# A Conformer mixer on one core: heads A in pairs of row halves, B's attention beside half of the output projection, norm factors on VectorE

## The chip, the cores and the metric

One Trainium2 chip, one core. The metric is the device time of one execution of the program, in microseconds. The trace comes from one profiled execution. Engines: PE is TensorE, PEld its weight loads, DVE VectorE, ACT ScalarE, POOL GpSimd; SP issues the loads.

## What is computed

One layer on a sequence of 512 tokens, width 1024, in float32:

```python
x = x + 0.5 * swiglu(rmsnorm(x), ffn1)
proj = rmsnorm(x) @ w_in                     # q, k, v of A (3 x 512), latents of B (256 + 128 + 32)
qa, ka = rmsnorm(heads of 64)                # A: 8 heads, bias by relative position, causal by chunks of 64
out_a = softmax(qa ka^T / 8 + bias) va
q  = rmsnorm(c_q) @ w_uq                     # B: 8 heads, 64 normed + 32 normed and rotated
kv = rmsnorm(c_kv) @ w_ukv                   # 64 of key, 64 of value; 32 rotated key columns are shared
out_b = softmax(q k^T / sqrt(96)) v          # the same chunk mask, no bias
x = x + concat(out_a, out_b) @ w_out
x = x + 0.5 * swiglu(rmsnorm(x), ffn2)
x = rmsnorm(x)
```

The feed-forward width is 2816. Every factor of a norm is 1 / sqrt(mean square + 1e-6).

## The kernel before

x is kept transposed, as 8 tiles of 128 columns by 512 tokens. Each matmul of float32 is made of three (`mm3`, L146 to L149): both operands are split into a high and a low part, and high x high, high x low and low x high are added in PSUM. The low part is made by a subtraction on DVE or POOL after a cast on ACT. Weights come in units of 128 x 1024 (`wunit`, L136): SP loads `raw`, ACT casts `whi`, POOL or DVE (`lo_on`) makes `wlo`; there are 4 buffers of each.

The mixer (L247 to L578) goes through these steps.

1. `in_proj` of the latents (L334), the factor of the row norm (L337 to L342), three latent norms with `factors` (L347 to L349).
2. `qk_proj` of qA (L377): 96 matmuls into four banks, squares on ACT, sums on DVE, `factors`, and a multiplication out of PSUM (L375). Then `latents_T`, B's queries (L384 to L404) and B's keys and values (L408 to L431), each with factors and scaling, with `rope` on POOL.
3. `qk_proj` of kA (L433), and `values_proj` for A (L566).
4. The heads, 8 of A and then 8 of B, in a software pipeline (L569 to L578). Iteration `it` flips the probabilities of head `it`, makes scores and softmax of head `it + 1`, prepares queries and keys of head `it + 2` (`front`), and multiplies the values of head `it - 1`. `front` transposes queries and keys on PE into the tag "tr", for A once for two heads, and splits them. `softmax` has four blocks of 128 queries with 512, 384, 256 and 256 columns: `mm3`, a reduction on DVE that adds the bias and finds the row's extreme (L522), an exponential on ACT (L524), a reciprocal on DVE (L525), a scaling on POOL (L526). `flip` (L529) transposes ten blocks into three banks of the tag "t" and splits them (L547, L548). A head of A has 64 rows: even heads lie in partitions 0 to 63, odd ones in 64 to 127.
5. After the pipeline, the output projection (L589 to L599): for each of 8 column blocks of x, 8 x 3 matmuls, a residual add (L595), a split for the second feed-forward part and a square sum. That part follows.

`rsqrt` (L112) is ln and exp on ACT and one Newton step of four DVE instructions. PSUM has eight banks; in the mixer 2 are for scores ("s"), 2 for transposes ("tr"), 3 for flips ("t") and 1 for values ("pv"). `bank` gives the projections four of them: group 0 is s, s, tr, tr and group 1 is t, t, t, pv.

The order on each engine is made by a planner (`schedule_with_timeline_sim`), which goes by the program's order, by its own estimate of each instruction's time and by priorities; `high_priority(offset=150)` moves the first fronts and softmaxes ahead (L572). Once it is made, each engine takes its instructions in that order. SP's queue holds the loads of weights and of the bias tables.

The lines that the steps below touch: L112 to L119, L276 to L289, L307 to L312, L358 to L433, L453 to L505, L507 to L527, L529 to L564, L569 to L578, L589 to L599.

Of the kernel before, what the change touches and what calls it, by code (L numbers as in the profile page):

```python
# [10 lines left out]
F32 = mybir.dt.float32  # L11
F32R = mybir.dt.float32r
AF = mybir.ActivationFunctionType
ALU = mybir.AluOpType
# [3 lines left out]
P = 128  # L18
# [12 lines left out]
BIG = 1e30  # L31

# [7 lines left out]
def tile_macaron_block(  # L40
# [206 lines left out]
    AH, AL = XH, XL  # L247
    with tc.tile_pool(name="mix", bufs=1, side="left", reuse_waits="tile") as mp:
        latT = mp.tile([P, 6, S], F32R, tag="vAh", name="latT")
        VBh = mp.tile([P, NT, 4, 192], F32R, tag="vBh", name="VBh")  # L250
# [22 lines left out]
        dve.tensor_scalar(out=nq[:, 0:1], in0=g(C_AQ), scalar1=-(HD ** -0.5), scalar2=None, op0=ALU.mult)  # L273
        dve.tensor_scalar(out=nq[:, 1:2], in0=g(C_BQ), scalar1=-(QK ** -0.5), scalar2=None, op0=ALU.mult)

        def factors(ss, n, width, scaled, name):  # L276

            f = mp.tile([P, NT, n], F32, tag="f_" + name, name="f_" + name)
            y = mp.tile([P, NT, n], F32, tag="y_" + name, name="y_" + name)
            y2 = mp.tile([P, NT, n], F32, tag="z_" + name, name="z_" + name)  # L280
            if scaled:
                dve.tensor_tensor(out=f, in0=ss, in1=vtok.unsqueeze(2).broadcast_to([P, NT, n]), op=ALU.mult)
                dve.tensor_scalar(out=f, in0=f, scalar1=1.0 / width, scalar2=EPS, op0=ALU.mult, op1=ALU.add)
            else:
                dve.tensor_scalar(out=f, in0=ss, scalar1=1.0 / width, scalar2=EPS, op0=ALU.mult, op1=ALU.add)
            rsqrt(f, f, y, y2)
            if scaled:
                dve.tensor_tensor(out=f, in0=f, in1=rtok.unsqueeze(2).broadcast_to([P, NT, n]), op=ALU.mult)
            return f  # L289
# [16 lines left out]
        with tc.tile_pool(name="ps2", bufs=1, space=PSUM, reuse_waits="tile") as ps:  # L306
            NB = {"s": 2, "tr": 2, "t": 3, "pv": 1}  # L307

            def bank(group, i, name):

                tag = (("s",) * NB["s"] + ("tr",) * NB["tr"], ("t",) * NB["t"] + ("pv",) * NB["pv"])[group][i]
                return ps.tile([P, 512], F32, tag=tag, name=name, bufs=NB[tag])  # L312

# [20 lines left out]
            pts = in_proj(0, LAT, 1)  # L334
            mt = bank(0, 3, "mt")
# [3 lines left out]
            yt = mp.tile([P, NT], F32, tag="yt", name="yt")  # L339
            zt = mp.tile([P, NT], F32, tag="zt", name="zt")  # L340
# [400 lines left out]
```

## Time and profile before

| | |
|---|---|
| median of 3 runs | 996.65 us (996.12 to 996.72) |
| the profiled execution | 997.57 us |
| its span, first to last instruction | 995.8 us |
| TensorE's mean granted clock | 0.994 of 2.4 GHz |
| PE busy | 975.5 us (98%) |
| DVE / ACT / POOL busy | 390.5 / 391.9 / 579.6 us |

The span is 1.8 us shorter than the execution's own time. Matmuls are pipelined and their ends are modelled, so a busy PE can still be slower than it might be; the starts are measured, and so are the gaps that a row calls idle. In a row, "<-" after the bracket's time names what ended the wait. The first feed-forward part lasts until about 368 us, the mixer with its output projection until 622 us, the second feed-forward part until the end.

### The profile page before, as it was taken

Reading aid. Unit: us, or ns where it says so; the run is one execution under the profiler, and the core shown is the slowest. Engines: PE = TensorE matmul, PEld = TensorE weight load, DVE = VectorE, ACT = ScalarE, POOL = GpSimd, SP = SyncE. Lnnn points to the kernel's source line nnn. Section 1 sums busy time; section 2 is a strip of 40 time slices with the busy share of each in tenths; the row PEclk is TensorE's granted clock in tenths of the full one; section 3 lists DMA queues with packets and bytes.
Section 4 is the critical chain, followed back from the end, with each engine's and each line's share of the span. In section 5 each row is a group of like instructions: output and inputs, shape, how many; then the busy total and the mean of one; then the engine's idle time right before and its main releaser. Section 6 shows DMA issues by size and latency. Waiting matters only on the chain.

```text
span 995.8 us, 12076 instructions
## 1 busy us (share of the span) xinstructions
PE 975.5 (98%) x4579; PEld 812.1 (82%) x4579; DVE 390.5 (39%) x684; ACT 391.9 (39%) x661; POOL 579.6 (58%) x424
## 2 busy tenths in 40 slices
PE   9999999999999999898999999999999999999996
PEld 6888888888888889786778978888888888888886
DVE  7533333333121233866788845143333333200002
ACT  7533323232222236563778853343233232322321
POOL 4776666765555530385445567587666667645541
PEclk9999999999999999999999999999999999999998
DMA  6432223233233242220110062323322232333302
GB/s 233 145 109 86 102 89 106 85 106 95 83 102 93 89 141 75 85 64 1 32 33 2 1 212 88 103 86 106 102 88 99 93 104 80 101 96 95 101 16 85
DMA packets 29146, 89.90 MB, mean 90 GB/s; under 512 B 3488, under 2 KB 5664, under 8 KB 29088
## 3 DMA queue, kind: packets, MB, share of 16 engines
q1 hardware_dynamic: 28224, 88.34, 27.6%
q8 instruction: 36, 0.59, 0.2%
q10 hardware_dynamic: 864, 0.79, 0.2%
q14 instruction: 22, 0.18, 0.1%
HBM read 87.02 MB, written 2.10 MB: 89 GB/s over the span
## 4 chain that ended last, share of the span: by engine, by line
PE 89%; DVE 4%; ACT 3%; POOL 2%; issue 1%; DMA 1%; SPq 0%; POOLq 0%; ACTq 0%; DVEq 0%
PE gu L147 15%; PE gu L149 15%; PE gu L148 15%; PE dn L147 8%; PE dn L149 8%; PE dn L148 8%; PE pj L149 2%; PE pj L147 2%; PE pj L148 2%; PE wo L147 1%; PE wo L149 1%; PE wo L148 1%; PE t L542 1%; PE s L147 1%; PE tr L457 1%
## 5 line engine op out<-in xcount | busy, mean ns | idle before, releaser
L143 POOL TENSOR_TENSOR wlo<-raw,whi 128x1024 fp32r<-128x1024 f32 x138 | 324.2, 2350 | 153.3 <-ACT whi L142 152.5
L142 ACT CAST whi<-raw 128x1024 fp32r<-128x1024 f32 (+2 forms) x159 | 162.4, 1022 | 447.7 <-PE gu L148 244.8
L147 PE MATMUL gu<-x2h,whi 128*128 128x512 f32 x352 | 136.9, 389 | 0.0
L148 PE MATMUL gu<-x2l,whi 128*128 128x512 f32 x352 | 136.8, 389 | 0.0
L149 PE MATMUL gu<-x2h,wlo 128*128 128x512 f32 x352 | 136.8, 389 | 0.0
L148 PE MATMUL gu<-xl,whi 128*128 128x512 f32 x320 | 124.5, 389 | 0.0
L147 PE MATMUL gu<-xh,whi 128*128 128x512 f32 x320 | 124.5, 389 | 0.0
L149 PE MATMUL gu<-xh,wlo 128*128 128x512 f32 x320 | 124.5, 389 | 0.0
L162 POOL TENSOR_TENSOR us<-us,gs 128x512 f32<-128x512 f32 x44 | 57.6, 1310 | 108.7 <-DVE us L160 107.2
L161 DVE SCALAR_TENSOR_TENSOR gs<-th,gs 128x512 f32<-128x512 f32 x44 | 91.1, 2074 | 31.8 <-ACT th L159 31.8
L158 DVE TENSOR_TENSOR gs<-gu,rs 128x512 f32<-128x512 f32 x44 | 30.4, 691 | 175.9 <-PE gu L149 168.7
L191 DVE SCALAR_TENSOR_TENSOR x<-dn,x 128x512 f32<-128x512 f32 (+1 forms) x17 | 11.2, 660 | 193.9 <-PE dn L149 193.9
L148 PEld LDWEIGHTS gu<-x2l,whi 128*128 128x128 f32 x352 | 66.1, 188 | 13.8
L149 PEld LDWEIGHTS gu<-x2h,wlo 128*128 128x128 f32 x352 | 66.1, 188 | 13.8
L147 PEld LDWEIGHTS gu<-x2h,whi 128*128 128x128 f32 x352 | 66.1, 188 | 13.6
L149 PEld LDWEIGHTS gu<-xh,wlo 128*128 128x128 f32 x320 | 60.1, 188 | 12.6
L147 PEld LDWEIGHTS gu<-xh,whi 128*128 128x128 f32 x320 | 60.1, 188 | 12.5
L148 PEld LDWEIGHTS gu<-xl,whi 128*128 128x128 f32 x320 | 60.1, 188 | 12.3
L147 PE MATMUL dn<-h1h,whi 128*128 128x512 f32 x176 | 68.5, 389 | 0.0
L148 PE MATMUL dn<-h1l,whi 128*128 128x512 f32 x176 | 68.5, 389 | 0.0
L149 PE MATMUL dn<-h1h,wlo 128*128 128x512 f32 x176 | 68.5, 389 | 0.0
L160 DVE SCALAR_TENSOR_TENSOR us<-gu,rs 128x512 f32<-128x512 f32 x44 | 30.4, 690 | 64.9 <-PE gu L149 64.9
(327 smaller groups left out, 1864.5 us busy)
## 6 DMA issues: line engine op xcount, KB each, us to landing
raw<-in_gu SPq DMA_DIRECT2D x84, 512.0 KB, 3.6
raw<-in_dn SPq DMA_DIRECT2D x32, 512.0 KB, 3.5
raw<-in_dn SPq DMA_DIRECT2D x16, 384.0 KB, 3.1
raw<-in_w_in SPq DMA_DIRECT2D x12, 512.0 KB, 3.4
raw<-in_w_out SPq DMA_DIRECT2D x8, 512.0 KB, 4.3
x<-in_xT SPq DMA_DIRECT2D x8, 256.0 KB, 5.4
raw<-in_gu SPq DMA_DIRECT2D x8, 256.0 KB, 5.4
bias<-in_bias_tab SPq DMA_DIRECT2D x8, 256.0 KB, 2.7
```

Of the source, the lines that this page charges most:

```text
L142: act.copy(hi[:, :n], raw[:, :n])
L143: (lo_on or pool).tensor_tensor(out=lo[:, :n], in0=raw[:, :n], in1=hi[:, :n].bitcast(F32), op=ALU.subtract)
L147: pe.matmul(out, lhsT=ah, rhs=bh, start=start, stop=False)
L148: pe.matmul(out, lhsT=ah, rhs=bl, start=False, stop=False)
L149: pe.matmul(out, lhsT=al, rhs=bh, start=False, stop=stop)
L158: dve.tensor_tensor(out=gs, in0=gup[0], in1=rs, op=ALU.mult)
L160: dve.scalar_tensor_tensor(out=us, in0=gup[1], scalar=0.5, in1=rs, op0=ALU.mult, op1=ALU.mult)
L161: dve.scalar_tensor_tensor(out=gs, in0=th, scalar=1.0, in1=gs, op0=ALU.add, op1=ALU.mult)
L162: pool.tensor_tensor(out=us, in0=us, in1=gs, op=ALU.mult)
L191: dve.scalar_tensor_tensor(out=x[dt][:, h], in0=pt[:, h], scalar=0.5, in1=x[dt][:, h], op0=ALU.mult, op1=ALU.add)
L457: pe.transpose(pt[0:src(t).shape[1], t * P:(t + 1) * P], src(t), ident)
L542: pe.transpose(tt[:, o + i * P:o + (i + 1) * P], pi[i][:, j * P:(j + 1) * P], ident)
```

## The change

1. `rsqrt_small` makes a first guess by integer arithmetic on the bits and takes three Newton steps, all on DVE: ten instructions. `factors` uses it and takes several norms at once: the three latent norms together, B's two query norms together. ACT's ln and exp remain in the feed-forward parts alone.
2. The pipeline's first four entries are pairs of A's heads. `softmax` makes the scores of both heads of a pair block by block, a matmul of the low half of the rows and then one of the high half. All four blocks have one reciprocal, and POOL scales them after it. The bias is loaded once a head as before, and its sign is put into the reduction (`scale=-1.0`), so that L482 goes. `pb` moves from the weight buffers into parts of `rs` and `ssum`.
3. `flip` fills its three banks one after the other, with the copies of each behind its transposes.
4. A's half of the output projection (`out_a`) runs in the iterations of B's heads, with its weights loaded in iterations 4 and 5 (`weights_o`) into the space of A's values and keys. B's half follows, with the first two column blocks begun before the last head's values (`out_b`). x gets two adds for each column block.
5. PSUM's eight banks: s 2, tr 1, t 2, pv 1, and 2 of a new tag pj, for second score tiles, B's keys and projections.

The diff, cut to its core:

```diff
+        def rsqrt_small(out, v, w):
+            y, t = (mp.tile([P, 2 * NT * NH], F32, tag="rsq", name="rsq", bufs=2)[:, 0:w] for _ in range(2))
+            dve.tensor_scalar(out=y.bitcast(I32), in0=v.bitcast(I32), scalar1=-0.5, scalar2=RSQ, op0=ALU.mult, op1=ALU.add)
+            for i in range(3):
+                dve.scalar_tensor_tensor(out=t, in0=y, scalar=-0.5, in1=y, op0=ALU.mult, op1=ALU.mult)
+                dve.tensor_tensor(out=t, in0=t, in1=v, op=ALU.mult)
+                dve.scalar_tensor_tensor(out=out if i == 2 else y, in0=t, scalar=1.5, in1=y, op0=ALU.add, op1=ALU.mult)
...
-            rsqrt(f, f, y, y2)
+            flat = f.rearrange("p i t n -> p (i t n)")
+            rsqrt_small(flat, flat, w)
...
-            NB = {"s": 2, "tr": 2, "t": 3, "pv": 1}
+            NB = {"s": 2, "tr": 1, "t": 2, "pv": 1, "pj": 2}
...
-                tag = (("s",) * NB["s"] + ("tr",) * NB["tr"], ("t",) * NB["t"] + ("pv",) * NB["pv"])[group][i]
+                tag = (("t", "t", "pv", "pj"), ("s", "s", "tr", "pj"))[group][i]
...
-            fcq = factors(ssl[:, 0], 1, 256, True, "cq")
-            fkv = factors(ssl[:, 1], 1, 128, True, "ckv")
-            fkr = factors(ssl[:, 2], 1, 32, True, "kr")
+            fcq, fkv, fkr = factors([(ssl[:, 0], 256), (ssl[:, 1], 128), (ssl[:, 2], 32)], 1, True, "lat")
...
+            def weights_o(i):
...
+                raw = wraw.tile([P, 1024], F32, tag="raw", name="raw")
+                nc.sync.dma_start(out=raw, in_=w_out[0, i])
+                act.copy(hi, raw)
+                pool.tensor_tensor(out=lo, in0=raw, in1=hi.bitcast(F32), op=ALU.subtract)
+                B["o", i] = hi, lo
+
+            def out_a(dt):
+                hi, lo = B["o", dt // 2]
+                pt = ps.tile([P, 512], F32, tag="pj", name="woa", bufs=NB["pj"])
+                for c in range(4):
+                    cc = slice((dt % 2) * 512 + c * P, (dt % 2) * 512 + (c + 1) * P)
+                    mm3(pt, hi[:, cc], lo[:, cc], OUT[c][0], OUT[c][1], c == 0, c == 3)
+                dve.tensor_tensor(out=x[dt], in0=pt, in1=x[dt], op=ALU.add)
...
-                    nc.sync.dma_start(out=bias, in_=bias_tab[h])
-                    dve.tensor_scalar(out=bias, in0=bias, scalar1=-1.0, scalar2=None, op0=ALU.mult)
-                    pool.memset(bias[0:HD, S - HD:S], BIG)
+                    nc.sync.dma_start(out=bias, in_=bias_tab[2 * pr + e])
+                    pool.memset(bias[0:HD, S - HD:S], -BIG)
...
-                    mm3(so[:, 0:nn], qh[:, ii], ql[:, ii], kh[:, 0:nn], kl[:, 0:nn], True, True)
...
-                    dve.reciprocal(sm[:, i:i + 1], sm[:, i:i + 1])
-                    pool.tensor_tensor(out=pi[i], in0=pi[i], in1=sm[:, i:i + 1].broadcast_to([P, (i + 1) * P]), op=ALU.mult)
+                    if i > 0:
+                        tag = "pj" if i == 2 and len(heads) > 1 else "s"
+                        bk = [ps.tile([P, 512], F32, tag=tag, name=f"s{i}", bufs=NB[tag]) for _ in heads]
+                    so = [b[:, 256:512] if i == 1 else b[:, 0:nn] for b in bk]
+                    for j, (a, b) in enumerate(((0, 2), (0, 3), (1, 2))):
+                        for o, hd in zip(so, heads):
+                            pe.matmul(o, lhsT=hd[a][:, ii], rhs=hd[b][:, 0:nn], start=j == 0, stop=j == 2)
...
+                for pi, mn, sm in out:
+                    dve.reciprocal(sm, sm)
+                    for i in (3, 2, 1, 0):
+                        pool.tensor_tensor(out=pi[i], in0=pi[i], in1=sm[:, i:i + 1].broadcast_to([P, (i + 1) * P]), op=ALU.mult)
...
+            beside = {}
+            for i in range(4):
+                beside.setdefault(4 + i // 2, []).append(lambda i=i: weights_o(i))
+            for dt in range(KD):
+                beside.setdefault(5 + min(dt, 6), []).append(lambda dt=dt: out_a(dt))
+            fronts = [lambda pr=pr: front_a(pr) for pr in range(4)] + [lambda b=b: front_b(b) for b in range(NH)]
+            n = len(fronts)
...
+                    if it == n:
+                        B["wb"] = wunit(w_out[1, 0], 1024)
+                        for dt in range(2):
+                            out_b(dt, 4, KD - 1)
...
+                    for f in more[e * half:(e + 1) * half]:
+                        f()
+            for dt in range(2):
+                out_b(dt, KD - 1, KD)
...
-            hi, lo = wunit(w_out[dt], 1024)
-            pt = ps.tile([P, S], F32, tag="mm", name="wo")
-            for c in range(KD):
+            if dt > 1:
+                if dt % 2 == 0:
+                    hi, lo = wunit(w_out[1, dt // 2], 1024)
+                pt = ps.tile([P, S], F32, tag="mm", name="wo")
+                for c in range(4, KD):
```

`w_out` is laid out anew on the host to match (two halves of four units of 128 x 1024).

## Rows read from the trace of the kernel before

**Rows 1.** The page's section 1: busy us, share of the span, instructions
```profile
PE 975.5 (98%) x4579; PEld 812.1 (82%) x4579; DVE 390.5 (39%) x684; ACT 391.9 (39%) x661; POOL 579.6 (58%) x424
```

**Rows 2.** Windows: length, busy us of PE, PEld, DVE, ACT, POOL, clock, DMA
```profile
405.00:420.00 15.00, 12.04 (x64) 10.29 (x63) 10.82 (x20) 10.92 (x18) 3.37 (x6) 1.00 0.37 123
420.00:461.00 41.00, 41.00 (x186) 34.42 (x186) 29.76 (x69) 22.57 (x50) 35.09 (x31) 1.00 0.12 39
461.00:470.00 9.00, 4.81 (x21) 3.92 (x20) 4.94 (x11) 2.87 (x4) 0.97 (x3) 0.81 0.00 0
...
482.00:521.00 39.00, 38.29 (x237) 29.12 (x235) 33.85 (x116) 29.81 (x87) 20.11 (x43) 1.00 0.15 42
521.00:578.60 57.60, 56.36 (x374) 49.91 (x373) 47.98 (x170) 47.45 (x135) 30.84 (x59) 1.00 0.10 34
```

**Rows 3.** Timeline, kA's chain: start us, us, engine, line, out<-in, idle before
```profile
459.51 1.20 DVE L283 TENSOR_SCALAR f_ka<-f_ka 128x32 f32<-128x32 f32 x1
...
460.99 1.28 ACT L115 ACT_TABLE_LOAD   x1
...
462.54 0.19 DVE L116 TENSOR_TENSOR z_ka<-y_ka 128x32 f32<-128x32 f32 x1 [1.83 <-ACT y_ka L115]
...
463.66 2.48 DVE L375 TENSOR_TENSOR kA<-pj,f_ka 128x512 f32<-128x512 f32 x4
...
465.70 1.08 PE L457 MATMUL tr<-ident,qA 128*128 128x128 f32 x4 [4.19 <-DVE kA L375]
```

**Rows 4.** Tile wo: count, duration ns min/median/max, first and last start us
```profile
L147 PE MATMUL wo<-xh,whi x64: 389/389/397, 579.3 to 622.1; 128*128 128x512 f32 x64
```

**Rows 5.** Timeline of PE, scores of single heads of A
```profile
482.44 0.38 PE L542 MATMUL t<-ident,pa 128*128 128x128 f32 x2
482.75 0.38 PE L147 MATMUL s<-qk,qk 64*128 64x256 f32 x1
...
483.30 0.44 PE L542 MATMUL t<-ident,pa 128*128 128x128 f32 x2
...
486.22 0.50 PE L147 MATMUL s<-xh,xh 64*128 64x512 f32 x1
...
487.12 0.66 PE L457 MATMUL tr<-ident,kA 128*128 128x128 f32 x4
```

**Rows 6.** Tile t of the flips, 470 to 578 us, as rows 4
```profile
L542 PE MATMUL t<-ident,pa x112: 270/273/332, 482.4 to 575.8; 128*128 128x128 f32 x112
...
L547 ACT CAST PBh<-t x32: 244/310/387, 485.0 to 577.7; 128x128 fp32r<-128x128 f32 x16, 128x256 fp32r<-128x256 f32 x16
...
L548 DVE TENSOR_TENSOR PBl<-t,PBh x31: 265/292/425, 486.5 to 576.9; 128x128 fp32r<-128x128 f32 x16, 128x256 fp32r<-128x256 f32 x15
```

**Rows 7.** Timeline, qA's chain
```profile
413.69 0.17 DVE L283 TENSOR_SCALAR f_qa<-f_qa 128x32 f32<-128x32 f32 x1
...
417.80 0.19 DVE L288 TENSOR_TENSOR f_qa<-f_qa,rtok 128x32 f32<-128x32 f32 x1
...
418.77 0.50 PE L147 MATMUL pj<-whi,xh 128*128 128x512 f32 x1 [1.24 <-DVE qA L375]
```

**Rows 8.** Timeline, POOL and DVE in kB's chain
```profile
452.54 1.29 POOL L303 TENSOR_TENSOR rtmp<-rtmp 128x512 f32<-128x512 f32 x1
452.66 1.22 DVE L117 TENSOR_TENSOR z_kn<-z_kn,f_kn 128x32 f32<-128x32 f32 x1
```

**Rows 9.** Timeline of PE, scores of two heads of A
```profile
493.11 0.49 PE L147 MATMUL s<-xh,xh 64*128 64x512 f32 x2
...
493.99 0.33 PE L542 MATMUL t<-ident,pb 128*128 128x128 f32 x1
```

**Rows 10.** Lines by form, DVE, 470 to 578 us: count, busy, mean ns
```profile
L525 DVE RECIPROCAL sm<-sm 128x1 f32<-128x1 f32 x64 | 9.0, 151 | 1.3 <-ACT pb L524 0.6 <-ACT pa L524 0.5
...
L482 DVE TENSOR_SCALAR bias<-bias 128x512 f32<-128x512 f32 x6 | 3.6, 594 | 0.9 <-DMA bias<-in_bias_tab 0.9
```

**Rows 11.** The page's section 5, POOL's low part of a weight unit
```profile
L143 POOL TENSOR_TENSOR wlo<-raw,whi 128x1024 fp32r<-128x1024 f32 x138 | 324.2, 2350 | 153.3 <-ACT whi L142 152.5
```

More of the change, by code (lines that the diff above doesn't have):

```diff
@@ new lines, in norm_k @@
+            def norm_k():
+                fk, = factors([(B["ssk"], HD)], NH, False, "kn")
+                for t in range(NT):
+                    dv = kB[:, t, :].rearrange("p (h w) -> p h w", w=HD)
+                    pool.tensor_tensor(out=dv, in0=dv, in1=fk[:, t, :].unsqueeze(2).broadcast_to([P, NH, HD]), op=ALU.mult)
+            tiles_b()
+            for j in range(3):
+                latents_T(j)
+            for i in range(8):
+                queries_b(i // 4, i % 4)
+            norm_q()
@@ L436, in values_proj @@
+            for i in range(8):
+                keys_values_b(i // 2, i % 2)
+            norm_k()
+            qk_proj(416 + 512, kA, "ka", 1)
             def values_proj():
@@ new lines, in values, with out_b @@
+                    act.copy(oh, pv)
+                    dve.tensor_tensor(out=ol, in0=pv, in1=oh.bitcast(F32), op=ALU.subtract)
+            def out_b(dt, c0, c1):
+                if c0 == 4:
+                    B["b", dt] = ps.tile([P, 512], F32, tag="pj", name="wob", bufs=NB["pj"])
+                pt, (hi, lo) = B["b", dt], B["wb"]
+                for c in range(c0, c1):
+                    cc = slice(dt * 512 + (c - 4) * P, dt * 512 + (c - 3) * P)
+                    mm3(pt, hi[:, cc], lo[:, cc], OUT[c][0], OUT[c][1], c == 4, c == KD - 1)
+                if c1 == KD:
+                    dve.tensor_tensor(out=x[dt], in0=pt, in1=x[dt], op=ALU.add)
@@ new lines, in tile_macaron_block @@
+            for it in range(-2, n + 1):
+                pis = prob.pop(it, [None])
+                more = beside.get(it, [])
+                for e, pi in enumerate(pis):
+                    cur = None
+                    if pi is not None:
+                        cur = head, flip(pi)
+                        head += 1
+                    if e == 0:
+                        with (tc.high_priority(offset=150) if it < 0 else ExitStack()):
+                            if 0 <= it + 1 < n:
+                                prob[it + 1] = softmax(qk.pop(it + 1))
+                            if it + 2 < n:
+                                qk[it + 2] = fronts[it + 2]()
+                    if it == n:
+                        B["wb"] = wunit(w_out[1, 0], 1024)
+                        for dt in range(2):
+                            out_b(dt, 4, KD - 1)
+                    if last:
+                        values(*last)
+                    last = cur
+                    half = (len(more) + 1) // 2 if len(pis) > 1 else len(more)
+                    for f in more[e * half:(e + 1) * half]:
+                        f()
```

290 lines of the change are left out of this document (142 added, 148 removed).

## The prediction

> **What bounds the kernel now.** First the busy shares of the page: PE runs for 98% of the span [rows 1], so time can only come from work taken off PE or from holes in its stream. Then the stretches of the mixer [rows 2], where the reader is to see how few holes there are and who stands beside them. PE has 3.0 us idle in 405 to 420 and 4.2 us in 461 to 470, and the granted clock of the latter is 0.81: (1 - 0.81) x 9 us x 2 = 3.4 us at the lower level (1.2 of 2.4 GHz), behind a hole of 4.19 us [rows 3], which costs another 1.7 us of work. From 482 to 578.6, the attention, PE looks full, but matmul ends are modelled, so I count its work. The 192 matmuls of the output projection, 512 columns each, keep one pace: 64 of one line from 579.3 to 622.1 us [rows 4], 42.8 us for 189 steps, 226 ns each. The columns of one head's values (512, 384, 256, 256, three matmuls each, 4224 in all) are then 1.87 us; 16 heads of values and 8 of B's scores make 45 us, some 245 transposes at 0.11 us (0.38 us for two [rows 5], 0.27 us for one [rows 6]) 27 us, A's scores about 16 us. That is 88 of 96.6 us: some 8 us idle, with DVE at 87% and ACT at 76% in A's part (482 to 521), both at 83% in B's.
>
> I take a step's chain of waits from the timeline and a stage's cost from its busiest engine.
>
> **1. Norm factors by Newton steps.** Each chain loses two ACT instructions, mostly with a table load of 1.28 us ahead [rows 3], and goes from four DVE steps to ten. A dependent step takes 0.22 us: five of them from 462.54 to 463.66 us [rows 3]. Two chains reach PE.
>
> For qA, DVE's L283 starts at 413.69 and L288 at 417.80 [rows 7]: 4.1 us. Ten steps behind L283 are 0.2 + 10 x 0.22 = 2.4 us, 1.7 us sooner, more than PE's wait of 1.24 us at 418.77 [rows 7]. **-1.2 us**; bounds -3.0 (the whole hole) and +0.8 (steps held by POOL, below).
>
> For kA the old hop over ACT began early, and ten steps save only 0.5 us: L283 of this chain ended at 460.7, L375 starts at 463.66 [rows 3], where it would start near 463.2. But the two merged chains before it (three of the latents, two of B's queries) also lose their loads, so POOL's rope and key scaling, which follow, end sooner, and the table loads no longer stand between ACT's squares and casts. PE sat in front of the transposes although the projection of A's values was ready; the planner had put these first by its own estimate of the chain, and a chain on one engine should miss its estimate by less. I take half the hole, and with it half the time at the lower clock: **-2.5 us**; bounds -5.9 (hole and clock) and +1.0.
>
> Here the row speaks against the change: DVE's L117 took 1.22 us instead of 0.19 and ended as POOL's L303 ended [rows 8]. So each Newton step can cost a POOL instruction. The Trainium skill says the same (SBUF — State Buffer, "SBUF: two separate sides"): DVE and GpSimd share a port pair as an exclusive lock, held for a whole instruction. By that rule alone the term would be a loss; this is the third rival.
>
> **2. A's heads in pairs.** A head's scores have 64 rows, and a pair now issues low half, high half, low half. The serial price: 0.90 us for three matmuls of 512 columns (486.22 to 487.12), 0.55 us for three of 256 (482.75 to 483.30) [rows 5]; 384 columns lie between, 0.72 us. A head: 0.90 + 0.72 + 2 x 0.55 = 2.72 us, eight 21.8 us. The old kernel already shows the overlap: a block of 512 columns of one head and one of 256 of another, six matmuls, took 0.88 us (493.11 to 493.99) [rows 9], not 1.45, and the timeline has this six times, so the scores cost some 18.4 us now. In pairs, 4 x 2.72 = 10.9 us. A change into the 64-row form costs about 0.1 us (0.31 us from two transposes at 482.44 to the score, where two steps are 0.22 [rows 5]); some nine fewer give 0.9 us. In all 8.4 us of PE work are gone.
>
> What of it reaches the time? DVE loses six of eight reciprocals a pair (0.151 us each) and two bias negations (0.594 us) [rows 10]: 2.1 us. About three pairs run in 482 to 521, so DVE falls from 33.85 to 27.7 us, PE by some 6.4 us to about 30, and ACT, unchanged at 29.8 us [rows 2], becomes the fullest. The fullest engine fills 87% of the stretch today; 29.8 / 0.87 = 34.3, so -4.7 us, and -1.1 us for the pair that lies outside the stretch (half its PE saving). **-5.8 us**; bounds 0 and -8.4.
>
> One reciprocal for all four blocks means that POOL scales a head only after its last exponential. POOL's queue is half empty here (20.1 of 39 us), and the flip of these probabilities comes an iteration later: nothing, unless that lead is used up. The bias loads keep their number on SP.
>
> **3. A's half of the output projection beside B's attention.** 96 matmuls, 21.7 us, move from behind the attention into it. With them go four weight loads on SP, their ACT casts and POOL lows (2.35 us each [rows 11]), and eight extra residual adds on DVE (as wide as L375, 2.48 us for four [rows 3]: 5.0 us). B's part has 57.6 us, about 5 of them idle on PE (its share of the 8). New demand: PE 57.6 - 5 + 21.7 = 74.3; DVE 48.0 + 5.0 - 3.6 (24 reciprocals) = 49.4; POOL 30.8 + 9.4; ACT's casts fit into its 10 us of slack. With the others at two thirds, the latencies that made the holes are covered, and at the drain the first two blocks of B's half stand in. **-4.5 us**; bounds -5 (every hole) and +2. An add that waits for its matmuls holds the score reductions queued behind it on DVE, and POOL's 9.4 us stand ahead of the scaling: that is the +2. In the projection that is left, POOL has one low and two square sums (the shape of L303, 1.29 us [rows 8]) for 5.4 us of matmuls, 4.9 us: full, but it has been ahead of PE by then, so 0.
>
> **4. Banks.** PSUM's tiles become 2 for scores, 1 (not 2) for transposed queries and keys, 2 (not 3) for flips, 2 shared ones for second score tiles, B's keys and projections. I charge nothing: other heads' matmuls stand between in the queue. If that cover is gone it is the slower rival.
>
> **Sum.** -1.2 - 2.5 - 5.8 - 4.5 = -14.0 us. The profiled execution took 997.57 us (span 995.8 and 1.8 around it), so 983.6; it lies 0.9 us above the median of 996.65, so in the runs' measure **982.6 us**.
>
> **Rivals.**
> *All holes close.* -3.0 - 5.9 - 8.4 - 5 = -22.3: 974.4 us. For it: each is a wait with a named releaser, and out_a is work without waits. Against: ACT and DVE don't become faster.
> *Evacuation, not PE, sets A's pace.* The matmuls of a pair finish earlier but exponentials and low parts come no sooner, or the planner doesn't alternate the halves; A gives -2 (the DVE share), B -3, the rest as above: -8.7, 988 us. For it: ACT's 29.8 us. Against: it had 9 us of slack. The Trainium skill has this as a rule (TensorEngine Tiling (Array Packing), "PSUM Bottleneck": packing speeds TensorE, not the emptying of PSUM). The 87% of DVE bears it out in part.
> *Newton steps behind POOL.* In 420 to 461 POOL is busy for 35.1 of 41 us and DVE for 29.8 [rows 2]. The chains of B's queries and keys lie there: some ten of their twenty steps meet a POOL instruction, 1.0 us each [rows 8]. DVE has 11 us to spare, but the reductions and low weights of kA queue behind; if some 7 us come through, -14 + 7 = -7: 989.6 us.
> *Slower: flips wait for their banks.* With two banks, the third tile of a flip waits until the first is copied: two ACT copies of 0.31 us and two DVE lows of 0.29 us [rows 6], 1.2 us, less the 0.33 us of the second tile's transposes, 0.87 us; 16 heads 14 us. The single bank between queries and keys adds at least the same 1.2 us for 4 pairs: 5 us. -14 + 19 = +5: 1001.6 us. It decides where over three quarters of that is exposed, 0.65 us a flip. Against: rows 5 show the transposes already cut up between other heads' scores.
>
> **Chances.** Forecast 0.52, all holes 0.12, evacuation 0.16, Newton behind POOL 0.10, slower 0.10. Below 0.2% (2 us) a measurement of this kernel can't tell a change from none. Faster 0.86: the first three, and most of the fourth; same 0.04; slower 0.10. The range goes from just under the second case to above the third and fourth, 972 to 993; some 0.07 lies below, 0.12 above.
>
> **What would show it.** Right: no table loads between 386 and 465; L288 of kA less than 2.6 us behind its L283; score matmuls of two heads starting within 0.02 us of each other; a pair of A in 11.5 to 12 us; PE without holes while projection matmuls stand in B's part. Wrong: Newton steps of 0.6 to 2 us; flips' transposes whose wait names L548; score matmuls of the two halves 0.2 us apart; a wait longer than 3 us ahead of kA's transposes with the clock at half behind it.

## The result, and the profile after

The changed kernel takes 1010.08 us (median of 4 runs, 1009.49 to 1012.39) against 996.68 us before on the same chip: a ratio of 1.0136 with a 95% interval of 1.0117 to 1.0156, so 1.4% slower. The forecast was 982.6 us. The profiled execution took 1012.39 us, with a span of 1010.5 us.

Section 1 of the page, of after, answers to [rows 1]; PE and DVE are busy for a little longer, ACT and POOL for less, and PE's share falls from 98% to 97%:

```profile
PE 984.3 (97%) x4579; PEld 817.7 (81%) x4579; DVE 393.6 (39%) x660; ACT 373.4 (37%) x629; POOL 573.8 (57%) x424
```

To find the loss, I cut each span at four marks: the first matmul of the mixer's input projection, the first transpose of A's queries, the fourth evacuation of values (the last of A), and the first matmul of the second feed-forward part. The windows between them, of before (start to end, length, busy time and count of PE, PEld, DVE, ACT and POOL, granted clock, DMA share, GB/s):

```profile
367.80:465.70 97.90, 90.75 (x435) 78.71 (x433) 62.44 (x157) 56.31 (x109) 48.40 (x55) 1.00 0.22 72
465.70:539.50 73.80, 72.54 (x423) 57.22 (x424) 56.82 (x191) 51.48 (x145) 31.86 (x65) 0.98 0.08 22
539.50:622.80 83.30, 82.61 (x458) 71.25 (x457) 55.08 (x130) 50.35 (x117) 55.79 (x58) 1.00 0.28 92
```

The same windows of after:

```profile
366.50:464.00 97.50, 91.75 (x441) 79.89 (x439) 70.51 (x179) 36.18 (x77) 44.37 (x55) 0.99 0.25 72
464.00:550.50 86.50, 82.82 (x428) 64.47 (x429) 53.45 (x159) 53.64 (x146) 32.25 (x65) 0.83 0.08 25
550.50:636.50 86.00, 81.80 (x448) 69.39 (x447) 50.22 (x112) 48.69 (x112) 48.90 (x53) 1.00 0.24 74
```

The projections are 0.4 us shorter, A's part is 12.7 us longer, the stretch from there to the second feed-forward part 2.7 us, and that part, to the end of the span, 1.0 us (374.0 after 373.0). The mixer starts 1.3 us earlier. Together 14.7 us, the difference of the spans.

A's part has a granted clock of 0.83. Two stretches of after at the lower level (1.2 of 2.4 GHz), with the one just ahead of the second:

```profile
459.00:469.00 10.00, 5.97 (x19) 4.62 (x18) 5.87 (x14) 0.69 (x1) 1.56 (x4) 0.66 0.00 0
476.00:482.60 6.60, 5.00 (x32) 3.40 (x31) 5.99 (x22) 5.89 (x18) 0.00 (x0) 1.00 0.00 0
482.60:506.50 23.90, 23.90 (x79) 16.90 (x80) 11.40 (x37) 12.18 (x36) 11.96 (x24) 0.50 0.15 45
```

The first is (1 - 0.66) x 10 x 2 = 6.8 us long, the second 23.9 us. Before there were 3.4 us [rows 2]. At the lower level matmuls of 512 columns start 0.43 us apart instead of 0.23 (after, 466.13 and 466.56 against 469.73 and 469.95 us), so about half of such time is lost wherever PE has work. In A's part lie 28.8 us of it now and 2.7 us before, the rest in the hole ahead of the transposes: an estimate of 14.4 us lost now, 1.4 then. That is the 12.7 us of A's part and a little more: without the lower clock, A's part would be 72.1 us, where that of before would be 72.4.

What PE did before the clock fell the second time is in the timeline of PE, of after (start, us, engine, line, operation, out<-in, count, idle before and its releaser):

```profile
463.97 1.08 PE L504 MATMUL tr<-ident,qA 128*128 128x128 f32 x4 [4.03 <-DVE kA L375]
...
472.91 0.60 PE L504 MATMUL tr<-ident,kA 128*128 128x128 f32 x4
...
475.42 0.39 PE L151 MATMUL pj<-whi,xl 128*128 128x512 f32 x1
475.74 1.49 PE L577 MATMUL s<-qk,qk 64*128 64x512 f32 x9
...
478.03 0.62 PE L577 MATMUL s<-qk,qk 64*128 64x256 f32 x3 [0.21 <-DVE mn L579]
479.03 1.27 PE L577 MATMUL s<-qk,qk 64*128 64x256 f32 x6 [0.38 <-DVE mn L579]
480.56 0.65 PE L504 MATMUL tr<-ident,kA 128*128 128x128 f32 x4 [0.27 <-DVE xl L509]
...
482.60 1.11 PE L577 MATMUL s<-xh,xh 64*128 64x512 f32 x3 [0.74 <-ACT xh L508]
```

Three things are to be seen. The hole ahead of the transposes is still there, 4.03 us (4.19 us before, [rows 3]). The keys of the first pair are transposed 8.9 us after its queries, when the projection of A's values is all but used up, so the scores start with nothing left beside them. And the first flip comes only at 487.80 us, 12.1 us after the first score; before it was 9.2 us (473.2 to 482.4). Between 475.7 and 487.8 us PE has scores and transposes alone, each waiting for its evacuation.

### The profile page after: what moved, and what is told of

Read it like the earlier page. It is cut to its first block, busy times and chain, and to the rows that moved or that the text cites. A ratio compares the mean times of both kernels' runs of the same rounds, so it can differ in the third digit from the quotient of the medians.

```text
span 1010.5 us, 12006 instructions
## 1 busy us (share of the span) xinstructions
PE 984.3 (97%) x4579; PEld 817.7 (81%) x4579; DVE 393.6 (39%) x660; ACT 373.4 (37%) x629; POOL 573.8 (57%) x424
## 5 line engine op out<-in xcount | busy, mean ns | idle before, releaser
L145 POOL TENSOR_TENSOR wlo<-raw,whi 128x1024 fp32r<-128x1024 f32 x134 | 315.1, 2353 | 141.4 <-ACT whi L144 138.3
L144 ACT CAST whi<-raw 128x1024 fp32r<-128x1024 f32 (+2 forms) x155 | 158.0, 1020 | 435.1 <-PE gu L150 242.1
L585 POOL TENSOR_TENSOR pa<-pa,sm 128x512 f32<-128x512 f32 (+2 forms) x48 | 35.6, 756 | 59.6 <-DVE sm L583 59.6
```

The costliest lines, as they stand in the source:

```text
L144: act.copy(hi[:, :n], raw[:, :n])
L145: (lo_on or pool).tensor_tensor(out=lo[:, :n], in0=raw[:, :n], in1=hi[:, :n].bitcast(F32), op=ALU.subtract)
L585: pool.tensor_tensor(out=pi[i], in0=pi[i], in1=sm[:, i:i + 1].broadcast_to([P, (i + 1) * P]), op=ALU.mult)
```

## The experiments

All times stand against runs of the kernel before on the same chip, 996.2 to 998.0 us by the batch. The time of a single run can be off by 1 to 3 us (four runs of e14 lay between 988.47 and 991.65, five of e9 between 999.19 and 1002.80), so kernels that ran once (e1 to e4, e6 to e8, e11, e12, e15, e18) are read by the stages of their profile. The stages of every kernel, cut as above; "half" is the time at the lower clock between the first and the last mark, in us. Stages and "half" are those of the one profiled execution:

| kernel | time | proj. | A | B | FFN2 | half |
|---|---|---|---|---|---|---|
| before | 996.68 | 97.9 | 73.8 | 83.3 | 373.0 | 3.4 |
| after | 1010.08 | 97.5 | 86.5 | 86.0 | 374.0 | 30.7 |
| e1_serial | 1006.1 | 97.5 | 80.1 | 85.9 | 374.6 | 17.1 |
| e2_k_on_pj | 1003.75 | 97.5 | 77.4 | 85.9 | 374.6 | 10.2 |
| e3_wo_behind | 1009.42 | 98.4 | 85.6 | 85.9 | 372.4 | 30.7 |
| e4_ln_exp | 1010.32 | 98.0 | 83.8 | 86.0 | 374.1 | 27.3 |
| e5_newton_alone | 997.83 | 97.7 | 73.9 | 85.1 | 372.4 | 3.4 |
| e6_key_norm_late | 1004.53 | 93.1 | 83.8 | 85.9 | 374.2 | 23.9 |
| e7_flip_banks_3 | 1004.45 | 97.8 | 72.9 | 90.2 | 375.2 | 20.4 |
| e8_k_pj_recip_by_block | 994.36 | 98.3 | 71.9 | 81.2 | 374.4 | 3.4 |
| e9_recip_by_block | 999.63 | 97.6 | 77.9 | 81.2 | 374.6 | 13.6 |
| e10_pairs_held_together | 1032.97 | 97.5 | 112.0 | 81.2 | 374.1 | 54.5 |
| e11_r_wo_behind | 1000.58 | 98.4 | 75.2 | 84.4 | 373.0 | 6.8 |
| e12_r_heads_singly | 997.23 | 98.4 | 74.0 | 81.2 | 374.0 | 6.8 |
| e13_pairs_ordered | 996.10 | 97.5 | 74.6 | 81.2 | 374.6 | 6.8 |
| e14_three_edits | 989.97 | 93.1 | 72.4 | 81.1 | 374.6 | 0 |
| e15_flip_banks_3_recip | 992.93 | 97.9 | 68.9 | 84.1 | 374.6 | 10.2 |
| e16_four_edits | 988.39 | 93.8 | 66.0 | 84.0 | 374.6 | 0 |
| e17_three_edits_ordered | 991.79 | 94.7 | 73.0 | 81.2 | 374.5 | 6.8 |
| e18_three_edits_wo_behind | 992.15 | 93.1 | 74.1 | 84.4 | 372.8 | 0 |

### First batch: which part brings the lower clock

e1 takes the alternation of the two heads inside a block out, e2 puts kA's transposes in the shared banks, e3 moves A's half of the output projection back, e4 takes the factors by ln and exp again, still merged.

```diff
-                    for j, (a, b) in enumerate(((0, 2), (0, 3), (1, 2))):
-                        for o, hd in zip(so, heads):
+                    for o, hd in zip(so, heads):
+                        for j, (a, b) in enumerate(((0, 2), (0, 3), (1, 2))):
```

> The changed kernel, but in each block of a pair the three matmuls of one head come first and then the three of the other (no alternation of the row halves). Theory ramp (PE falls to half clock from 482.6 to 506.5 us because the scores of the first pairs stand behind A's values projection, with nothing else to multiply): the stretch at half clock stays, 15 us or more of it, and the time is 1009 to 1016 us. Rival rows (two 64-row matmuls beside each other are what lets the clock fall): the stretch at half clock is under 7 us and the time falls to 998 to 1003 us. Rival banks (flips wait for their two banks, the clock is a side effect): within 3 us of 1010.

```diff
-                evac(kh, kl, transposes(lambda t: kA[:, t, hs]), g(C_AK))
+                evac(kh, kl, transposes(lambda t: kA[:, t, hs], "pj"), g(C_AK))
```

> The changed kernel, but the transposed keys of A go into a bank of pj and no longer into the single bank tr behind the queries. Theory ramp: kA's transposes follow qA's at once, scores of the first pair mix with the values projection as in the kernel before, the time at half clock in 470 to 510 us falls from 24 to under 7 us, and the kernel takes 997 to 1002 us. Rival rows: half clock for 15 us or more all the same, 1006 us or more. Rival banks: 1007 to 1012 us, with the waits of values and flips for the copies as they are.

```diff
-            for dt in range(KD):
-                beside.setdefault(5 + min(dt, 6), []).append(lambda dt=dt: out_a(dt))
...
+            for c in range(KD):
+                hi, lo = wa[c // 4]
```

> The changed kernel without its third part: nothing of the output projection beside the attention, all of it after the last head (each x gets one add). A's part up to 520 us should stay as it is, half clock included, in every theory. If the move is worth what the prediction charged, 1014 to 1016 us; if it is worth nothing or costs (the adds on DVE and POOL's low parts in front of the softmax), 1005 to 1011 us.

```diff
-            dve.tensor_scalar(out=y.bitcast(I32), in0=v.bitcast(I32), scalar1=-0.5, scalar2=RSQ, op0=ALU.mult, op1=ALU.add)
...
+            rsqrt(out, v, y, t)
```

> The changed kernel with the norm factors by ln and exp on ACT and one Newton step again, still merged. Rival of the prediction, Newton steps behind POOL (four steps of the kA chain took 1.0 us each behind the scaling of kB): the hole ahead of kA's transposes (4.0 us) shrinks by 2 us or more, the half clock behind it shortens from 6.8 to 3.4 us, 1004 to 1008 us. If the chains cost the same both ways, 1008 to 1012 us.

e2 is the one that says most alone: 6.3 us. With a bank of their own, kA's transposes follow qA's at once, the first score comes at 471.6 instead of 475.7 us, beside the projection of A's values, and 30.7 us at the lower clock become 10.2. Its A part fell by 9.1 us. Behind 470 us 6.8 us at the lower clock are left, as theory ramp has it; the time lies 1.75 us above that theory's range. That the order of the heads in a block (e1) changes the clock as well, by 13.6 us of stretch, shows how little it takes at the start of the attention. e1's time and stretch fit none of its three theories: 1006.1 us, with 13.6 us at the lower clock behind the start. e3 and e4 changed nothing that can be measured: neither the moved projection nor the Newton steps by themselves bring the loss, and the hole ahead of the transposes was 4.26 us with ln and exp. Both times lie where their theory of no gain and no loss has them.

### Second and third batch: one part alone, and the reciprocal

e5 is the kernel before with the Newton factors and nothing else of the change; the new function and its calls are those of the diff above.

> The kernel before with the Newton factors alone (each chain by itself, the old order of the work, the old banks, heads singly). If the Newton steps are a gain and only the new order and banks lose (theory 'ramp and banks'): 993 to 996 us, no lower clock beyond the one 3.4 us stretch. If the steps held behind POOL cost time in themselves (theory 'Newton behind POOL'): 998 to 1001 us, with the hole ahead of the first transposes longer than the 4.19 us of before.

It took 997.83 us, a ratio of 1.0009 (0.9999 to 1.0019): no gain and hardly a loss, between both theories. Its stages are those of before within 0.2 us up to the end of A's part; B's part is 1.8 us longer in its profile and FFN2 0.6 us shorter. The hole ahead of its first transposes is 4.46 us, longer than the 4.19 us of before, as the second theory has it.

```diff
-            norm_k()
             qk_proj(416 + 512, kA, "ka", 1)
+            norm_k()
```

> The changed kernel with the norm factors and the scaling of B's keys issued behind the projection of kA instead of ahead of it, so that POOL's 4.05 us scaling no longer stands beside kA's Newton steps. Theory 'Newton behind POOL': the steps go from 1.0 to about 0.2 us, the hole ahead of the transposes shrinks from 4.03 to about 1 us, the stretch at half clock at 462 goes, and the time is 1004 to 1007 us. Theory 'the one tr bank and the evacuations empty PE at the change of stage': the hole goes, but the clock still falls near 480 for 10 us or more, and the time is 1007 to 1010 us.

The hole went, as the first theory has it, and the projections shrank by 4.4 us to 93.1. The clock then fell at 473.4 us for 23.9 us, as the second has it; the time, 1004.53 us, lies in the range of the first. Its first flip comes 12.1 us after its first score, exactly as in after.

```diff
-            NB = {"s": 2, "tr": 1, "t": 2, "pv": 1, "pj": 2}
+            NB = {"s": 2, "t": 3, "pv": 1, "pj": 2}
...
-            def transposes(src, tag="tr"):
+            def transposes(src, tag="pj"):
```

> The changed kernel with three banks for the flips again and none of its own for transposed queries and keys (these go to the two shared banks, where the score tiles of 384 columns, B's keys and the projections are). Theory 'flips wait for their two banks': waits of flip transposes for their copies nearly gone, B's part 4 to 6 us shorter, 1002 to 1006 us. Theory 'flips are late because their probabilities are': waits of flip transposes stay at over half, 1007 to 1012 us.

The time fits the first theory, but not by its mechanism: the gain is in A's part, 13.6 us, of which less time at the lower clock explains some 7.6, and B's part became 4.2 us longer, with two stretches of 3.4 us at the lower clock in it.

```diff
                         act.activation(pi[i], pi[i], AF.Exp, bias=mn[:, i:i + 1], scale=-1.0, accum_out=sm[:, i:i + 1])
-                for pi, mn, sm in out:
-                    dve.reciprocal(sm, sm)
-                    for i in (3, 2, 1, 0):
+                        dve.reciprocal(sm[:, i:i + 1], sm[:, i:i + 1])
                         pool.tensor_tensor(out=pi[i], in0=pi[i], in1=sm[:, i:i + 1].broadcast_to([P, (i + 1) * P]), op=ALU.mult)
```

> The changed kernel with kA's transposes in the shared banks (1003.75 us by itself) and the reciprocal and the scaling again block by block instead of once behind all four exponentials. Theory 'the probabilities come late because of the one reciprocal': stalls in B's part fall from about 14 to 9 us and the time is 998 to 1001 us. Theory 'banks': B's part as it was, 1003 to 1005 us, the added reciprocals of DVE costing up to 1 us.

> The changed kernel with one edit: reciprocal and scaling block by block again, as in the kernel before (kA's transposes stay on the single tr bank). Theory 'the one reciprocal behind all four exponentials makes the probabilities late': most of the 9.4 us that this edit gave on top of kA's transposes in the shared banks (1003.75 to 994.36 us) is its own, so 999 to 1002 us, with the drain of B's part (last evacuation of values to the second FFN's first matmul, 18.8 us) about as it is and stalls in B's part near 8.5 us instead of 15. Theory 'the two edits only help together, because each keeps PE fed in the ramp': 1005 to 1010 us, with half clock for 15 us or more behind the ramp.

This is the largest single cause. e8 fell from 1003.75 to 994.36 us, below the ranges of both its theories, and e9, with this edit alone, takes 999.63 us, a ratio to before of 1.0042 (1.0024 to 1.0060): 10.5 us less than the changed kernel by the medians, 9.4 us by the two ratios, although DVE does 48 reciprocals more. The first theory of e9 held in its time.

The edit acts at two places. At the start of the attention the first flip comes at 481.6 us, 6.4 us after the first score instead of 12.1, and the stretch at the lower clock that follows lasts 10.2 instead of 23.9 us. That distance doesn't set the stretch by itself: in e2 it is 14.2 us with 6.8 us at the lower clock behind it, in before 9.2 us with none, and in both the scores start beside the projection of A's values.

In B's part the edit takes 4.8 us away, always the same: of the kernels with two flip banks and A's projection beside the attention, all seven with the reciprocal by block have 81.1 or 81.2 us there, and all that have the single one 85.9 or 86.0. With the whole projection behind the attention it is another matter: 85.9 us with the single reciprocal (e3, 3.4 us of them at the lower clock) and 84.4 with those by block (e11), so next to nothing beyond the clock.

The 4.8 us are in the drain. From the last score to the second feed-forward part's first matmul after takes 33.5 us (602.97 to 636.47), e9 28.5 (594.81 to 623.26). Timeline of after, last head of B:

```profile
603.88 0.40 ACT L581 ACTIVATE pa<-pa,mn 128x128 f32<-128x128 f32 x1
...
604.63 0.17 DVE L583 RECIPROCAL sm<-sm 128x4 f32<-128x4 f32 x1
...
604.91 0.50 PE L149 MATMUL pv<-PAh,VBh 128*128 128x512 f32 x1 [1.10 <-ACT PAh L605]
604.94 1.83 POOL L585 TENSOR_TENSOR pa<-pa,sm 128x512 f32<-128x512 f32 x2 [2.31 <-DVE sm L583]
...
607.29 0.40 POOL L585 TENSOR_TENSOR pa<-pa,sm 128x128 f32<-128x128 f32 x1
...
607.45 0.71 PE L603 MATMUL tp<-ident,pa 128*128 128x128 f32 x5
...
609.43 0.44 PE L603 MATMUL tp<-ident,pa 128*128 128x128 f32 x2 [1.17 <-DVE PAl L606]
```

The reciprocal stands behind the last of the four exponentials, POOL then scales all four blocks one after the other, and the flips begin as the last of it runs. The flips wait for their two banks, and the last values and the waiting block of the output projection stand behind. In e9 (timeline of POOL) the same four scalings are spread out:

```profile
587.12 1.04 POOL L583 TENSOR_TENSOR pa<-pa,sm 128x512 f32<-128x512 f32 x1 [0.57 <-DVE sm L582]
...
591.30 0.83 POOL L583 TENSOR_TENSOR pa<-pa,sm 128x384 f32<-128x384 f32 x1
592.09 0.61 POOL L583 TENSOR_TENSOR ssum<-ssum,sm 128x256 f32<-128x256 f32 x1
...
596.45 0.40 POOL L583 TENSOR_TENSOR pa<-pa,sm 128x128 f32<-128x128 f32 x1 [3.75 <-DVE sm L582]
```

Waits of PE in 550 to 623 us (waited for: us in total, times, longest), of after:

```profile
PE pv L149 <- ACT PAh L605: 1.6, 2, 1.1
PE tp L603 <- DVE PAl L606: 1.2, 1, 1.2
PE wob L149 <- ACT xh L621: 0.9, 1, 0.9
```

and of e9, all there is:

```profile
PE pv L149 <- ACT PAh L603: 0.2, 1, 0.2
PE pv L150 <- DVE PAl L604: 0.2, 1, 0.2
```

### The pairs

```diff
+                    with (tc.tile_critical() if len(heads) > 1 else ExitStack()):
                         for j, (a, b) in enumerate(((0, 2), (0, 3), (1, 2))):
```

> The kernel with both edits (kA's transposes in the shared banks, reciprocal block by block; 994.36 us) and the six matmuls of each pair of score tiles kept together in PE's queue, low half, high half in turn. A's scores took 18.54 us of PE before and still take 15.86 us here, because the planner cuts the pairs up. Theory 'the pairs are not issued together, so the saving of work is not made': A's scores fall to 11 to 12 us and the time to 988 to 991 us. Theory 'evacuation sets A's pace': scores fall as much but the time stays at 993 to 996 us, with the difference as holes of PE in A's part.

A miss. The block held PE back until other engines were through, as the waits of PE in 470 to 560 us say, so it tells nothing of the pairs:

```profile
PE s L578 <- POOL bias L526: 7.3, 2, 3.7
PE s L578 <- ACT pa L582: 5.1, 3, 2.2
```

With A's part 112.0 us and 54.5 us at the lower clock it shows what a starved start costs.

```diff
-                    with (tc.tile_critical() if len(heads) > 1 else ExitStack()):
+                    with (tc.manual_schedule(engines={mybir.EngineType.PE}) if len(heads) > 1 else ExitStack()):
```

> The kernel with both edits (kA's transposes in the shared banks, reciprocal block by block; 994.36 us), with PE's six matmuls of a pair of score tiles bound to the order low half, high half in turn, other work free to stand between them (the block of the run before this one also held PE back for other engines, so it doesn't tell). Theory 'the planner issues the two heads one behind the other, so the saving of work is not made': A's scores fall from 15.86 to 11 to 13 us and the time to 989 to 992 us. Theory 'evacuation sets A's pace': scores fall but the time stays at 993 to 996 us or rises, since a pair now has to wait until both its banks are free.

> The kernel with both edits (994.36 us) and A's heads one by one again, each in its own iteration, everything else of the change kept. Theory 'the pairs are worth what their scores save on PE' (18.54 to 15.86 us): 996 to 999 us. Theory 'the pairs cost, since two heads share the banks and come in bursts': 988 to 993 us.

The changed kernel's PE timeline has its pairs cut up, here a head of 512 columns by itself, 0.89 us for three matmuls:

```profile
514.57 0.50 PE L577 MATMUL s<-xh,xh 64*128 64x512 f32 x1
514.91 0.39 PE L577 MATMUL s<-xl,xh 64*128 64x512 f32 x1
515.15 0.39 PE L577 MATMUL s<-xh,xl 64*128 64x512 f32 x1
515.46 0.50 PE L149 MATMUL pv<-PAh,VAh 128*128 128x512 f32 x1
```

In e13 both heads of such a block, six matmuls, take 0.90 us (495.75 to 496.65):

```profile
495.75 0.50 PE L578 MATMUL s<-xh,xh 64*128 64x512 f32 x2
496.09 0.40 PE L578 MATMUL s<-xl,xh 64*128 64x512 f32 x2
496.32 0.39 PE L578 MATMUL s<-xh,xl 64*128 64x512 f32 x2
496.65 0.42 PE L504 MATMUL tr<-ident,kpe 128*96 128x128 f32 x2
```

Summed over all 96 matmuls, from the start of each run of them to the start of what follows, A's scores took 18.54 us before; in after 9.93 us for the 18176 of 33792 columns at full clock, so 18.5 us for all; 15.86 us in e8; and in e13 12.02 us for 28416 columns, so 14.3 us. The figures for after and e13 are scaled up from the columns at full clock. The saving of work is there for whoever holds the order. The time is not: e13 took 996.10 us (ratio 0.9997, 0.9987 to 1.0007) against 994.36 of the one run of e8. That is the time of e13's second theory. Where the saving went is in the windows of A's part, of e8 and e13, then of e17 (whose twin without the order is e14, below):

```profile
465.10:537.00 71.90, 68.33 (x429) 54.49 (x430) 54.29 (x189) 52.22 (x146) 32.36 (x65) 1.00 0.10 30
462.80:537.40 74.60, 68.89 (x429) 54.20 (x430) 54.95 (x189) 52.83 (x146) 32.83 (x65) 0.95 0.09 29
462.80:535.90 73.10, 67.42 (x431) 53.06 (x430) 55.24 (x193) 52.66 (x147) 36.83 (x69) 0.98 0.09 30
```

e13 has 6.8 us at the lower clock there and e8 none. Counted as 3.4 us lost, that leaves PE 65.5 us of work instead of 68.3, 2.8 us less; 2.1 us of it came back as holes (5.7 us idle instead of 3.6), and the clock took more than the rest. For e17 against e14 the same estimate gives 2.8 us less work, 1.8 us more idle and 1.7 us lost to the clock. The holes are what "evacuation sets A's pace" expects, but without the clock A's part would have gained 0.7 us in e13 and some 1 us in e17. How much of the missing time is evacuation and how much the clock, these runs don't settle. e12, A's heads singly, was 2.9 us slower than e8, 2.1 of them in A's part and of these 1.7 by 3.4 us more at the lower clock: what the pairs give beyond the clock, in the order that the planner made, is about 0.4 us.

### A's half of the output projection

The edit is that of e3, in the kernels with two and with three edits.

> The kernel with both edits (994.36 us) and the whole output projection behind the attention again. Theory 'A's half of the projection fills holes of B's part once the probabilities come in time': 997 to 1000 us. Theory 'it moves work and fills nothing' (as in the changed kernel, where moving it back gave -0.7 us): 993 to 996 us.

> The kernel with three edits (989.97 us) and the whole output projection behind the attention again, as a second look at what A's half of it beside B's attention is worth where the probabilities come in time (first look: 994.36 to 1000.58 us). Theory 'it fills holes': 994 to 998 us. Theory 'it fills nothing': 989 to 992 us.

Behind the attention the projection makes A's and B's parts together 159.6 us in e11 against 153.1 in e8, of which 1.7 us are clock, and 158.5 in e18 against 153.5 in e14. So beside the attention it gains 5 us there, and loses 1.4 to 1.8 us in FFN2. The times, of single runs but for e14, say 6.2 and 2.2 us; e11's lies just above the range of its first theory, e18's between its two. In the changed kernel (e3) moving it back gave 0.7 us: what the projection filled, the drain behind the late probabilities took.

### What beats both kernels

e14 has three edits: kA's transposes in the shared banks, the reciprocal by block, the norm of B's keys behind kA's projection. e15 has three flip banks and the reciprocal by block, e16 the late norm as well, and e17 is e14 with the order of e13.

> The kernel with both edits (994.36 us), and the norm factors and scaling of B's keys issued behind the projection of kA. Theory 'POOL's scaling ahead of kA's Newton steps costs the hole, and only the hole' : the hole of about 3 us ahead of the transposes goes, no stretch at half clock follows, 990 to 992 us. Theory 'a shorter ramp uncovers the early attention' (as in the run with this edit alone, where half clock then lasted 23.9 us): 997 us or more, with half clock behind 473.

> Three banks for the flips, queries and keys in the shared banks, and the reciprocal block by block. Theory 'flips wait for their two banks' also when the probabilities come in time: 988 to 992 us. Theory 'two banks are enough once the probabilities come in time': 994 to 998 us.

> The kernel with three edits (989.97 us) and three flip banks. If the gain of the third flip bank with late probabilities out of the way (994.36 to 992.93 us) adds to it: 987 to 990 us. If what that gained was only another order of the ramp, which the late norm of B's keys changes anyway: 990 to 994 us.

> The kernel with three edits (989.97 us) and the pairs' matmuls bound to their alternate order. Theory 'evacuation sets A's pace' (the order alone took 1.3 to 3 us of PE work away and gave no time): 989 to 992 us, the saved work as holes. Theory 'PE sets it once the ramp is fed': 986 to 989 us.

e14 takes 989.97 us, a ratio to before of 0.9941 (0.9921 to 0.9960). Its windows:

```profile
365.40:458.60 93.20, 91.47 (x440) 79.86 (x440) 65.75 (x172) 36.23 (x77) 42.20 (x51) 1.00 0.25 76
458.60:531.00 72.40, 68.53 (x431) 54.55 (x430) 55.25 (x196) 52.25 (x147) 36.50 (x69) 1.00 0.10 30
```

The clock is 1.00 throughout, with no hole ahead of the transposes. With the late norm e6 alone fell to the lower clock for 23.9 us; with the probabilities in time and the keys in their own bank, it doesn't. That is the first theory of e14. e15's one run, 992.93 us, lies between its two theories.

e16 takes 988.39 us, 0.9920 (0.9903 to 0.9938), the best of all; its interval overlaps that of e14, so the third flip bank's own 1.6 us isn't shown by the times. Its A part of 66.0 us is shorter by 6.4, its B part longer by 2.9: 3.5 us less in the two together, where neither profile has any lower clock. So the choice of banks (two for the flips and one for queries and keys, or three and none) does cost something, though little shows as flips that wait for theirs. e17 took 991.79 us, 1.8 us more than e14: again the order of the pairs gives no time.

## Why the prediction was wrong

**The reciprocal: the step that failed most.** The prediction saw that POOL scales a head only after its last exponential, and took "nothing, unless that lead is used up". It measured +10.5 us (e9 against after; +9.4 by the ratios). The lead of one iteration doesn't exist for the first pair, where nothing else is there to do, nor for the last head, where nothing comes behind to cover.

**Term 1.** For qA, -1.2 us was right in kind: the part up to the end of kA's projection is 1.6 us shorter (366.5 to 446.2 us, 79.7; before 367.8 to 449.1, 81.3). For kA, -2.5 us had the wrong sign, beyond its bound of +1.0. (By its own rule, half of the hole and half of the clock's 1.7 us, the term should have read -2.95.) From the end of kA's projection to the transposes it is now 17.8 us (446.2 to 464.0) instead of 16.6: +1.2, and the longer stretch at the lower clock behind the hole, 4.9 us of it in A's part instead of 2.7, adds an estimated +1.1. The failing sentence is that POOL's key scaling would end sooner and so help. It comes just then. Timeline of DVE and POOL, of after:

```profile
456.23 4.05 POOL L447 TENSOR_TENSOR kB<-kB,f_kn 128x512 f32<-128x512 f32 x4 [2.89 <-DVE f_kn L286]
456.29 1.01 DVE L282 TENSOR_SCALAR rsq<-f_ka 128x32 int32<-128x32 int32 x1
457.34 0.98 DVE L284 SCALAR_TENSOR_TENSOR rsq<-rsq 128x32 f32<-128x32 f32 x1
458.35 0.97 DVE L285 TENSOR_TENSOR rsq<-rsq,f_ka 128x32 f32<-128x32 f32 x1
459.36 0.97 DVE L286 SCALAR_TENSOR_TENSOR rsq<-rsq 128x32 f32<-128x32 f32 x1
...
460.36 0.19 DVE L284 SCALAR_TENSOR_TENSOR rsq<-rsq 128x32 f32<-128x32 f32 x1
```

Four steps cost 1.0 us each beside POOL's scaling, the other six 0.19: 3.2 us of the hole's 4.03. Ln and exp in their place leave a hole of 4.26 us (e4), so what removes it is moving B's key norm, POOL's scaling with it, out of the way (e6, e14). The row cited against the change [rows 8] was the right one, but I looked for its victims in B's chains, not in kA's. These are two of the signs that the prediction named for being wrong: steps of 0.6 to 2 us, and a wait over 3 us with the clock at half behind it. In e14, where POOL's scaling comes later (timeline of DVE):

```profile
453.42 0.18 DVE L282 TENSOR_SCALAR rsq<-f_ka 128x32 int32<-128x32 int32 x1
453.63 0.19 DVE L284 SCALAR_TENSOR_TENSOR rsq<-rsq 128x32 f32<-128x32 f32 x1
```

The Trainium skill's rule of the shared port pair (SBUF — State Buffer, "SBUF: two separate sides") fits: a DVE instruction with two inputs in SBUF and a GpSimd instruction that reads SBUF take that pair in turn, each for its whole length. Here the trace agrees for the three such steps (L284, L285, L286), 0.97 to 0.98 us beside POOL and 0.19 us without; the first step, L282 with one input, was held as well, 1.01 us. And e5 shows that the Newton steps in the old order are worth nothing as a whole, where -3.7 us were counted: -1.6 us up to the end of kA's projection and +1.4 us from there to the transposes. There POOL caught the step just ahead of the ten (L296, 2.38 us), and the ten took 0.19 us each.

**Term 2.** The price of a pair was read rightly (0.90 us for six matmuls of 512 columns, e13). That it would be paid was not: the planner cut the pairs up, and of the 7.5 us that the scores were to lose (the other 0.9 of the 8.4 us weren't measured) none was gone in after (18.54 to 18.5 us), 2.7 us in e8, 4.2 us in e13. And where the work went, the time didn't follow (e13, e17). The second rival, at 0.16, named both: evacuation sets A's pace, "or the planner doesn't alternate the halves". The second is what happened in after. The Trainium skill's "PSUM Bottleneck" (TensorEngine Tiling (Array Packing)), by which tiling speeds up TensorE and not the emptying of PSUM, spoke for the first. The holes of e13 and e17 agree with it, about 2 of 2.8 us, but the lower clock took part of the saving too.

**Term 3.** -4.5 us was about right as a size, 5 us in the attention (e8 against e11, e14 against e18), but FFN2 gives 1 to 2 us back, which was charged at nothing: of after, PE's only wait in 636 to 660 us, the start of that part,

```profile
PE gu L150 <- DVE x2l L691: 1.3, 1, 1.3
```

**Term 4.** Banks were charged at nothing, since "other heads' matmuls stand between in the queue". At the start of the attention none do. The one tr bank cost 6.3 us by the time (e2), 9.1 us in A's part, almost all by the clock; the slower rival had it at 5 us, for waits and not for the clock. Its other half, 14 us of flips waiting for their banks, didn't come: those waits are 1.6 us in 470 to 625 us, though three flip banks, with queries and keys in the shared ones, made A's and B's parts 3.5 us shorter (e16 against e14).

**The sum.** Taken back one by one: 1010.1 us, 999.6 with the reciprocal by block, 994.4 with kA in the shared banks, 990.0 with the late norm. What the prediction lacked is that its terms meet at one place, the first 25 us of the attention, where each small lateness empties PE and the lower clock multiplies it. It priced the clock once, for one hole.

## What to carry to other kernels

Price a batched step (one reciprocal for four blocks) at the first and the last iteration, where no lead covers it: in the middle it cost nothing that shows (PE was busy for all but 0.02 of the 52.5 us from 550.5 to 603.0), at the ends it cost some 10 us of 1010. Before moving a chain from ACT to DVE, look which POOL instruction runs at that time on the chain that PE waits for, and move that out of the way first. And where the start of a stage is thin, charge the granted clock: 1.6 us of idle time in 6.6 us, no gap of it over 0.74 us, was followed by 24 us at half speed here.

## What the runs showed of the hardware

The lower clock can last long: in after PE was busy for 5.00 of 6.60 us before it fell at 482.6 us, and for all of the 23.9 us that it then stayed at the lower level. What starts and what ends such a stretch isn't settled by these runs. In e13 two matmuls on the two halves of the rows start 3 to 7 ns apart and take no longer than one (six of 512 columns 0.90 us, three of one head alone 0.89), but only when they stand side by side in PE's queue. A DVE step of 0.19 us took 1.0 us beside each of POOL's scalings of 128 x 512.
